# The low-part matmuls of an input projection, run between the high-part matmuls of the next weight unit

## The chip, the cores and the metric

The kernel runs on one core of one Trainium2 chip. The metric is the device time of one execution in microseconds (us). Three executions of the kernel before the change took 1726.51 to 1726.67 us, with a median of 1726.62 us.

## The reference

The kernel computes one decoder block in fp32 for a single sequence of 256 tokens and a model width of 2048. Two feed-forward layers of width 5632, each added at half weight, stand around a mixer. The mixer has two branches, a gated linear recurrence (LRU) and a short gated convolution, and both take their columns from one input projection `w_in` of 2048 x 5120.

```python
x = x + 0.5 * swiglu_ffn(rms_norm(x, ffn1_norm), ffn1_w_gate, ffn1_w_up, ffn1_w_down)
z = rms_norm(x, mix_norm) @ w_in                  # 256 x 2048 @ 2048 x 5120
lru_x, lru_gate, sc_b, sc_c, sc_x = split(z, 5)   # 1024 columns each
xc = causal_depthwise_conv(lru_x, lru_conv_w) + lru_conv_b
h = rg_lru(xc, lru_w_a, lru_b_a, lru_w_i, lru_b_i, lru_lambda)   # two 128x128 gates per head, then a scan
y_lru = h * gelu(lru_gate)
y_sc = sc_b * causal_depthwise_conv(sc_c * sc_x, sc_conv_w)
y = concatenate([rms_norm(y_lru, lru_out_norm), rms_norm(y_sc, sc_out_norm)])
x = x + y @ w_out
x = x + 0.5 * swiglu_ffn(rms_norm(x, ffn2_norm), ffn2_w_gate, ffn2_w_up, ffn2_w_down)
return rms_norm(x, final_norm)
```

The change touches the second line alone.

## The kernel before

**Products in parts.** Every fp32 product is made of passes in the format fp32r. A weight tile is split into a high part, which ScalarE (ACT) rounds to fp32r in two casts of 128x1024, and a low part, which VectorE (DVE) computes as raw minus high in one subtraction of 128x2048. The activations are split the same way. What is summed is high x high, high x low and low x high.

**Units.** A unit is 4 k-tiles of 128 rows by 512 columns of a weight: one load of 1 MB (`load`, L185, issued on SyncE's DMA queue), one pair of tiles for its parts (`split_tiles`, L198, from the pool `splits` of L78 with two buffers for high and two for low), the casts and the subtraction (`parts_of`, L214). The raw tiles come from the pool `raws` with three buffers (L81). `unit` (L221) is load and split together.

**The input projection.** `columns` (L331) computes 512 columns of z, transposed: the weight block is stationary, and the activations move. Four PSUM banks `ps_in`, one for each group of 128 columns, are filled from four units, 2048 rows in all. The activation tile `xT[u]` (called `xT_nm` in the profile) has 512 columns for each k-tile: the 256 tokens' high part and, beside it, their low part. So one high-part matmul moves 512 columns and gives high x high in the first half of the bank and high x low in the second; a low-part matmul moves the first 256 columns only and adds low x high to the first half. The two halves are added when the bank is emptied (`halves`, L992, and the additions after it). A unit has 16 high-part matmuls (4 k-tiles x 4 banks) and 16 low-part matmuls; before the change, all 16 high ones run and then all 16 low ones.

**The order of the columns.** The loop at L1216 calls `columns` eight times, by the list `order` of L1210: `in_0_0`, `in_0_1`, `in_1_0`, `in_4_0`, `in_1_1`, `in_4_1`, `in_2_0`, `in_2_1`. The function named in the list (`lru_x`, `lru_gate`, `sc_x`, `sc_b`) empties the four banks after each call. The 1024 columns of sc_c aren't made by `columns`: between the first and the second call stands a square product in seven products instead of eight (`sc_c`, L1145, through `seven`, L417; its tiles are named `in_c`). Its units of `w_in` are added to and subtracted from each other by DVE before they are split, and the parts of these go through the same two-buffered pool, except that every third pair of tiles comes from another pool there (L201). The products themselves are written by `multiply` (L228). Its results are copied out by `snap` (L443, the tiles `v_snap` and others) and combined on DVE. The emptying of the first call's banks (`half_x`, then the convolution in `xc`) is written behind its third product, by `between`.

**What lies between units.** Small pieces of later work (gates, convolutions, norms) are put on a list with a cost (`defer`, L61), and `pump(1.9)` at the end of each unit in `columns` lets pieces out until 1.9 us are spent. In the first call, the piece let out behind unit 0 holds the transposes of the last eight 128x128 blocks of the activations (`pt_nm`). In the second call, `first` runs behind unit 0 what the square product left to do (`turn`, L1153). A piece can hold small matmuls of its own, such as those of the LRU gates (`tha`, `thi` are ACT's reading of their banks).

**Who decides the order.** TensorE runs its instructions in the order written. For DVE and ACT a scheduler reorders within what the dependences allow, when the kernel is built; only the DMA issues on SyncE are held in the order written (L58, `sp.held`). Each engine then works through its queue in order. All eight PSUM banks come from one rotating pool (L83). All instructions go through one wrapper, so that the profile gives L43 as the line of almost all of them; tiles are told apart by their names.

Of the kernel before, what the change touches and what calls it, by code (L numbers as in the profile page):

```python
# [16 lines left out]
P = 128  # L17
D = 2048
S = 256
FF = 5632  # L20
NT = S // P
KD = D // P
KF = FF // P
CW = 512
NC_D = D // CW
UK = 4
# [23 lines left out]
def hybrid_block(ctx: ExitStack, tc: tile.TileContext, a: dict, out: bass.AP):  # L50
    nc = tc.nc
    Engine.pinned = False
    dve, act, pe, sp = (Engine(tc, e) for e in (nc.vector, nc.scalar, nc.tensor, nc.sync))
    sp.held = True
    x = a["x"][0]
# [12 lines left out]
    def pump(budget):  # L68

        owed[0] = min(owed[0], 0.0) + budget  # L70
        while pending and owed[0] > 0:
            cost, fn = pending.popleft()
            fn()
            owed[0] -= cost
# [10 lines left out]
    def bank(name):  # L85
        return psum.tile([P, 512], F32, tag="ps", name=name)
# [98 lines left out]
    def load(src, name, pieces=((0, UK),), loaded=None, kept=False):  # L185
        if kept and extra[0] is not bigs:
            raw = extra[0].tile([P, UK, CW], F32, tag="kept", name=f"raw_{name}", bufs=2)
        elif kept:
            raw = bigs.tile([P, UK, CW], F32, tag="big", name=f"raw_{name}")
        else:  # L190
            raw = raws.tile([P, UK, CW], F32, tag="raw", name=f"raw_{name}")
        for i, e in pieces:
            sp.dma_start(raw[:, i:e, :], src[i * P : e * P].rearrange("(j p) c -> p j c", p=P))
            if loaded:
                loaded(i)
        return raw

    def split_tiles(name):  # L198
        pool, bufs = splits, 2
        if extra:  # L200
            turn_of["split"] += 1  # L201
            if turn_of["split"] % 3 == 0:
                if extra[0] is bigs:
                    return [big(f"{part}_{name}") for part in ("hi", "lo")]
                pool, bufs = extra[0], 1
        return [pool.tile([P, UK, CW], F32R, tag=part, name=f"{part}_{name}", bufs=bufs) for part in ("hi", "lo")]

    def low_part(raw, hi, lo):
        dve.tensor_tensor(lo, raw, f32(hi), op=ALU.subtract)

    def blocks(hi, lo):
        return [(hi[:, j, :], lo[:, j, :]) for j in range(UK)]

    def parts_of(raw, name):  # L214
        hi, lo = split_tiles(name)
        for h in (slice(0, 2), slice(2, UK)):
            act.copy(hi[:, h, :], raw[:, h, :])
        low_part(raw, hi, lo)
        return blocks(hi, lo)

    def unit(src, name):  # L221
        return parts_of(load(src, name), name)
# [107 lines left out]

    def columns(w, c0, xT, name, first=None):  # L331
        ps = [bank(f"ps_{name}_{f}") for f in range(4)]
        for u in range(KD // UK):
            blk = unit(w[u * UK * P : (u + 1) * UK * P, c0 : c0 + CW], f"{name}_{u}")
            for part in range(2):
                for j in range(UK):
                    x = xT[u][:, j, :]
                    for f in range(4):
                        wf = blk[j][part][:, f * P : (f + 1) * P]
                        if part == 0:  # L340
                            pe.matmul(ps[f], wf, x, start=u == 0 and j == 0, stop=False)
                        else:
                            end = u == KD // UK - 1 and j == UK - 1
                            pe.matmul(ps[f][:, :S], wf, x[:, :S], start=False, stop=end)
            if u == 0 and first:
                first()
            pump(1.9)
        return ps
# [3 lines left out]
    def product(w, c, us, y, name, stagger=False, between=None):  # L352
        ps = [bank(f"ps_{name}_{t}") for t in range(NT)]
        cs = slice(c * CW, (c + 1) * CW)
        late = []
        for i, u in enumerate(us):
            blk = unit(w[u * UK * P : (u + 1) * UK * P, cs], f"{name}_{u}")
            begin, end = i == 0, i == len(us) - 1
            if stagger and i >= len(us) - 2:
                late.append((u, blk, begin, end))  # L360
            else:
                multiply([(ps[t], stationary(y(u), t), begin, end) for t in range(NT)], blk)
            if between:
                between(i)
            pump(1.5)

        for t in range(NT):
            for i, (u, blk, begin, end) in enumerate(late):
                if t < NT - 1:
                    multiply([(ps[t], stationary(y(u), t), begin, end)], blk)  # L370
                elif not end:
                    multiply([(ps[t], stationary(y(u), t), begin, i == len(late) - 2)], blk)
                else:
                    for o in (slice(0, CW // 2), slice(CW // 2, CW)):
                        ps.append(bank(f"ps_{name}_last")[:, : CW // 2])
                        multiply([(ps[-1], stationary(y(u), t), True, True)], [(h[:, o], l[:, o]) for h, l in blk])
        return ps
# [4 lines left out]
    def seven_of(sf, x0, x1, v, spare, parts, meanwhile=None):  # L382

        a11, a12, a21, a22 = v[0, 0], v[0, 1], v[1, 0], v[1, 1]
        parts = dict(zip((4, 5, 6, 2), parts))
        quads = {4: spare, 5: a11, 6: a21, 2: a12}
        sf.update({0: stationary(x0, 0), 1: stationary(x1, 0), 3: stationary(x1, 1)})

        def high(i):
            hi, lo = parts[i]
            act.copy(hi, quads[i])
            sf[i] = [(hi[:, j, :], lo[:, j, :]) for j in range(UK)]

        def low(i):
            hi, lo = parts[i]
            dve.tensor_tensor(lo, quads[i], f32(hi), op=ALU.subtract)

        def two():  # L400
            dve.tensor_tensor(a21, a11, a21, op=ALU.subtract)
            dve.tensor_tensor(a11, spare, a11, op=ALU.subtract)

        def last():
            dve.tensor_tensor(a12, a12, a11, op=ALU.subtract)

        dve.tensor_tensor(spare, a21, a22, op=ALU.add)
        high(4)
        if meanwhile:
            meanwhile()  # L410
        low(4)
        return two, last, high, low
# [4 lines left out]
    def seven(w, rows, cols, sf, xs, name, keep, done, between=None, early=False, own=None, factor=None):  # L417
# [33 lines left out]
        def product_of(i, raw, ps, begin=False, end=True, blk=None):  # L451
            multiply([(ps, sf[i], begin, end)], blk or parts_of(raw, f"{name}_p{i}"), True)

        def usual(i, raw, n, *targets, first=None):

            blk = first or parts_of(raw, f"{name}_x{i}{n}")
            if own:
                last = i == len(xs) - 1
                targets = [(apart[t, n], t, i == 0, last) for t in range(NT)]
            multiply([(ps, stationary(xs[i][1], t), b, z) for ps, t, b, z in targets], blk, True)  # L460
            if own and last:
                for t in range(NT):
                    own(t, n, apart[t, n])
# [509 lines left out]
    with tc.tile_pool(name="mixer", bufs=1, side="left") as mp, tc.tile_pool(name="mixw", bufs=2, side="left") as mw:  # L973
# [242 lines left out]
        for i, (use, part, half) in enumerate(order):  # L1216
            ps = columns(w_in, part * (D // 2) + half * CW, nm.xT, f"in_{part}_{half}", behind)
            behind = None
            if i == 0:
                flush()  # L1220
                nm.factor()
                nm.diagonals()
                nm.rows()
                bc = nm.bc
                behind = sc_c(lambda: use(ps, half))
                gate_weights("a", a["lru_w_a"][0])
                gate_weights("i", a["lru_w_i"][0])
                yT += [big(f"yT_{u}") for u in range(KD // UK)]
            else:
                use(ps, half)  # L1230
# [11 lines left out]
        for g in range(2):  # L1242
            if g == 1:
                flush()
            ps = product(w_out, 0, (2 * g, 2 * g + 1), yT.__getitem__, f"o0_{g}")
# [11 lines left out]
    with tc.tile_pool(name="outs", bufs=1, side="left") as op:  # L1257
# [10 lines left out]
        two, last_sum, high, low = seven_of(so, yT[0], yT[1], quads, spare, halves_of)  # L1268
# [9 lines left out]
        for g in range(2):  # L1278
            ps = product(
                w_out, 3, (2 * g, 2 * g + 1), yT.__getitem__, f"o3_{g}",  # L1280
                between=lambda i: [fn() for fn in steps[g, i]],
            )
# [122 lines left out]
```

## Time and profile before

| what | value |
|---|---|
| median of 3 executions | 1726.62 us |
| lowest and highest | 1726.51 and 1726.67 us |
| span of the profiled execution | 1725.0 us |
| what lies between the span and the median | 1.62 us |
| input projection with the square product, on TensorE | 705.8 to 933.9 us of the span |
| high-part matmuls of `columns` | 512, moving 512 columns each |
| low-part matmuls of `columns` | 512, moving 256 columns each |
| high-part casts on ACT (`hi_in`) | 64, 1045 ns each |
| low-part subtractions on DVE (`lo_in`) | 32, 2288 ns each |

The profile is one execution taken by the hardware profiler. PE is TensorE's matmuls, PEld its weight loads, which run beside the matmuls; DVE, ACT and POOL are VectorE, ScalarE and GpSimd, and SP is SyncE. An entry such as `ps_in<-xT_nm,lo_in x512` is a group of instructions by what they write and read, and how many they are. In a timeline, each row is a run of like instructions on an engine: start in us from the start of the span, length from the first start to the last end, engine, line, operation and tiles, shapes and count; a bracket gives the idle time before the row and what ended it. The recorded duration of a matmul includes its way through the array and overlaps the next one's, so that the step from one matmul to the next is read from starts, not from durations.

### The profile page before, as it was taken

The numbers are of one execution on the slowest core, as the hardware profiler recorded it, in microseconds if no ns is written. First come the engines' busy times: TensorE is split into PE (matmuls) and PEld (weight loads), VectorE is DVE, ScalarE is ACT, GpSimd is POOL, SyncE is SP. The second block draws the span as 40 slices with busy tenths as digits, with TensorE's granted clock in tenths as the row PEclk, the third lists the DMA queues.
The fourth block names the chain that finished last, engine by engine and source line by source line (L and its number), as shares of the span: only waits on it lengthen the run. The fifth ranks groups of instructions, "written<-read, shape, count | busy, mean of one in ns | idle before, by whom it ended". The sixth has DMA issues, their size and how long they took to land.

```text
span 1725.0 us, 20330 instructions
## 1 busy us (share of the span) xinstructions
PE 1715.1 (99%) x7985; PEld 1432.9 (83%) x7985; DVE 1509.3 (87%) x1239; ACT 1077.6 (62%) x1406; POOL 7.0 (0%) x34
## 2 busy tenths in 40 slices
PE   9999999999999999999999999999999999999998
PEld 8888888888888888888888888888888888888886
DVE  7998999889789898787897989889899887899896
ACT  7666566656466656666965657655556654656664
POOL 0100000000000000000000000000000000000000
PEclk9999999999999999999999999999999999999999
DMA  8574665566466656545566574665665646555743
GB/s 302 190 243 140 208 229 185 207 226 219 157 217 198 202 178 219 195 154 190 175 196 205 190 241 140 204 233 192 205 213 195 220 146 220 195 195 195 256 150 131
DMA packets 174223, 343.22 MB, mean 199 GB/s; under 512 B 5684, under 2 KB 8624, under 8 KB 174000
## 3 DMA queue, kind: packets, MB, share of 16 engines
q1 hardware_dynamic: 173632, 340.81, 58.5%
q8 instruction: 62, 1.02, 0.2%
q10 hardware_dynamic: 176, 1.06, 0.2%
q14 instruction: 33, 0.27, 0.0%
q0 software_dynamic: 320, 0.07, 0.0%
HBM read 339.82 MB, written 2.10 MB: 198 GB/s over the span
## 4 chain that ended last, share of the span: by engine, by line
PE 99%; DVE 0%; ACT 0%; DVEq 0%; issue 0%; ACTq 0%
PE ps_d L43 14%; PE ps_in L43 10%; PE ps_g_a L43 9%; PE ps_u_a L43 9%; PE ps_u_c L43 6%; PE ps_g_c L43 6%; PE ps_d_a L43 5%; PE ps_u_d L43 5%; PE ps_g_d L43 5%; PE ps_d_c L43 3%; PE ps_u_e L43 3%; PE ps_g_e L43 3%; PE ps_g L43 3%; PE ps_o L43 3%; PE ps_u L43 3%; PE ps_d_d L43 3%
## 5 line engine op out<-in xcount | busy, mean ns | idle before, releaser
L43 ACT CAST hi_g_p<-raw_g 128x1024 fp32r<-128x1024 f32 (+1 forms) x139 | 142.5, 1057 | 104.9 <-DVE raw_g L43 34.2
L43 DVE TENSOR_TENSOR lo_g_p<-raw_g,hi_g_p 128x2048 fp32r<-128x2048 f32 x70 | 159.5, 2285 | 31.6 <-ACT hi_g_p L43 31.3
L43 ACT CAST hi_u_p<-raw_u 128x1024 fp32r<-128x1024 f32 x140 | 141.4, 1050 | 68.1 <-DVE raw_u L43 24.7
L43 DVE TENSOR_TENSOR lo_u_p<-raw_u,hi_u_p 128x2048 fp32r<-128x2048 f32 x70 | 159.2, 2285 | 18.8 <-ACT hi_u_p L43 18.3
L43 PE MATMUL ps_d<-hi_d,h 128*128 128x512 f32 x696 | 166.0, 390 | 0.0
L43 PEld LDWEIGHTS ps_d<-hi_d,h 128*128 128x128 f32 x696 | 130.0, 188 | 26.6
L43 ACT CAST hi_d<-raw_d 128x1024 fp32r<-128x1024 f32 x88 | 88.6, 1048 | 68.3 <-PE ps_u_d L43 20.2
L43 DVE TENSOR_TENSOR lo_d<-raw_d,hi_d 128x2048 fp32r<-128x2048 f32 x44 | 100.6, 2289 | 28.9 <-ACT hi_d L43 28.9
L43 ACT CAST hi_d_p<-raw_d 128x1024 fp32r<-128x1024 f32 x84 | 85.3, 1050 | 61.2 <-DVE raw_d L43 42.2
L43 PE MATMUL ps_in<-xT_nm,hi_in 128*128 128x512 f32 x512 | 122.5, 391 | 0.0
L43 PEld LDWEIGHTS ps_in<-xT_nm,hi_in 128*128 128x128 f32 x512 | 94.1, 188 | 18.8 <-ACT tha L43 0.5
L43 ACT CAST hi_g_x<-raw_g 128x1024 fp32r<-128x1024 f32 (+1 forms) x79 | 81.5, 1059 | 39.4 <-PE ps_g_c L43 24.8
L43 ACT CAST hi_u_x<-raw_u 128x1024 fp32r<-128x1024 f32 x80 | 80.5, 1047 | 36.5 <-PE ps_u_c L43 20.0
L43 DVE TENSOR_TENSOR lo_d_p<-raw_d,hi_d_p 128x2048 fp32r<-128x2048 f32 x42 | 95.6, 2285 | 6.0 <-ACT hi_d_p L43 5.8
L43 DVE TENSOR_TENSOR raw_u<-raw_u,raw_u 128x2048 f32<-128x2048 f32 x40 | 91.6, 2289 | 9.5 <-DMA raw_u<-in_ffn_w_up_dram 8.8
L43 DVE TENSOR_TENSOR raw_g<-raw_g,raw_g 128x2048 f32<-128x2048 f32 x40 | 91.5, 2286 | 7.2 <-DMA raw_g<-in_ffn_w_gate_dram 6.8
L43 DVE TENSOR_TENSOR lo_g_x<-raw_g,hi_g_x 128x2048 fp32r<-128x2048 f32 x40 | 91.3, 2284 | 6.7 <-ACT hi_g_x L43 6.5
L43 DVE TENSOR_TENSOR lo_in<-raw_in,hi_in 128x2048 fp32r<-128x2048 f32 x32 | 73.2, 2288 | 26.5 <-ACT hi_in L43 26.0
L43 DVE TENSOR_TENSOR lo_u_x<-raw_u,hi_u_x 128x2048 fp32r<-128x2048 f32 x40 | 91.4, 2284 | 0.3
L43 PE MATMUL ps_d<-lo_d,h 128*128 128x512 f32 x348 | 86.2, 389 | 0.0
L43 ACT CAST hi_in<-raw_in 128x1024 fp32r<-128x1024 f32 x64 | 64.0, 1045 | 24.9 <-PE ps_in L43 15.4
L43 PEld LDWEIGHTS ps_d<-lo_d,h 128*128 128x128 f32 x348 | 65.3, 188 | 13.6
(471 smaller groups left out, 3737.6 us busy)
## 6 DMA issues: line engine op xcount, KB each, us to landing
raw_d<-in_ffn_w_down_dram SPq DMA_DIRECT2D x88, 1024.0 KB, 5.2
raw_u<-in_ffn_w_up_dram SPq DMA_DIRECT2D x87, 1024.0 KB, 5.3
raw_g<-in_ffn_w_gate_dram SPq DMA_DIRECT2D x86, 1024.0 KB, 5.3
raw_in<-in_w_in_dram SPq DMA_DIRECT2D x32, 1024.0 KB, 5.1
raw_in_c<-in_w_in_dram SPq DMA_DIRECT2D x8, 1024.0 KB, 5.3
raw_o<-in_w_out_dram SPq DMA_DIRECT2D x8, 1024.0 KB, 5.2
raw_o_q<-in_w_out_dram SPq DMA_DIRECT2D x8, 1024.0 KB, 5.2
xres<-in_x_dram SPq DMA_DIRECT2D x3, 512.0 KB, 9.3
```

The source lines that it names most:

```text
L43: ins = getattr(self.engine, name)(*args, **kwargs)
```

## The change

In `columns`, the sixteen low-part matmuls of a unit no longer follow its own sixteen high-part matmuls. They are held back and run between the high-part matmuls of the next unit: high 1 of unit u, low 1 of unit u-1, high 2 of unit u, low 2 of unit u-1, and so on. Unit 0's high-part matmuls run alone, since there is no unit before them, and the low part of unit 3 runs alone at the end. The number of matmuls, their operands and the loads stay the same. The calls of `first` and `pump` stay at the end of each unit's step, so that what they issue behind unit 0 now comes ahead of unit 0's low-part matmuls. Nothing is changed in the square product or in the other products, and the pools keep their sizes; `parts_of` is cut in two so that the tiles can be used as they are.

```diff
-    def parts_of(raw, name):
+    def split(raw, name):
         hi, lo = split_tiles(name)
         for h in (slice(0, 2), slice(2, UK)):
             act.copy(hi[:, h, :], raw[:, h, :])
         low_part(raw, hi, lo)
-        return blocks(hi, lo)
+        return hi, lo
+
+    def parts_of(raw, name):
+        return blocks(*split(raw, name))
+
+    def whole(src, name):
+        return split(load(src, name), name)
...
     def columns(w, c0, xT, name, first=None):
         ps = [bank(f"ps_{name}_{f}") for f in range(4)]
-        for u in range(KD // UK):
-            blk = unit(w[u * UK * P : (u + 1) * UK * P, c0 : c0 + CW], f"{name}_{u}")
-            for part in range(2):
-                for j in range(UK):
-                    x = xT[u][:, j, :]
-                    for f in range(4):
-                        wf = blk[j][part][:, f * P : (f + 1) * P]
-                        if part == 0:
-                            pe.matmul(ps[f], wf, x, start=u == 0 and j == 0, stop=False)
-                        else:
-                            end = u == KD // UK - 1 and j == UK - 1
-                            pe.matmul(ps[f][:, :S], wf, x[:, :S], start=False, stop=end)
+        n = KD // UK
+        before = []
+
+        def high(u, hi):
+            for j in range(UK):
+                x = xT[u][:, j, :]
+                for f in range(4):
+                    pe.matmul(ps[f], hi[:, j, f * P : (f + 1) * P], x, start=u == 0 and j == 0, stop=False)
+                    yield
+
+        def low(u, lo):
+            for j in range(UK):
+                x = xT[u][:, j, :S]
+                for f in range(4):
+                    end = u == n - 1 and j == UK - 1
+                    pe.matmul(ps[f][:, :S], lo[:, j, f * P : (f + 1) * P], x, start=False, stop=end)
+                    yield
+
+        for u in range(n):
+            hi, lo = whole(w[u * UK * P : (u + 1) * UK * P, c0 : c0 + CW], f"{name}_{u}")
+            for _ in high(u, hi):
+                if before:
+                    next(before[0])
+            before = [low(u, lo)]
+            if u == n - 1:
+                for _ in before[0]:
+                    pass
             if u == 0 and first:
                 first()
             pump(1.9)
```

## The prediction

> **What bounds the kernel now.** I read the page first: the span, the busy shares and the chain that ended last.
>
> ```profile
> span 1725.0 us, 20330 instructions
> PE 1715.1 (99%) x7985; PEld 1432.9 (83%) x7985; DVE 1509.3 (87%) x1239; ACT 1077.6 (62%) x1406; POOL 7.0 (0%) x34
> ...
> PE 99%; DVE 0%; ACT 0%; DVEq 0%; issue 0%; ACTq 0%
> ```
>
> TensorE is the path from end to end. Whatever the change does, it does by shortening the step from one matmul to the next, or by making TensorE wait. The profiled span of 1725.0 us lies 1.62 us under the median of the runs, 1726.62 us; I work out a difference against the span and add it to the median.
>
> Next the view by tile of the projection's PSUM tiles. Columns: shortest/median/longest in ns, then first and last start.
>
> ```profile
> L43 PE MATMUL ps_in<-xT_nm,hi_in x512: 387/389/499, 705.8 to 931.8; 128*128 128x512 f32 x171
> L43 PEld LDWEIGHTS ps_in<-xT_nm,lo_in x512: 187/192/192, 709.2 to 933.7; 128*128 128x128 f32 x171
> L43 PE MATMUL ps_in<-xT_nm,lo_in x512: 277/283/283, 709.4 to 933.8; 128*128 128x256 f32 x171
> ```
>
> These durations overlap, so they are not steps. A step is read from the timeline of PE (start us, length of the merged row, count), as the distance between starts of rows:
>
> ```profile
> 704.00 1.98 PE L43 MATMUL ps_d<-lo_d,h 128*128 128x512 f32 x8
> 705.81 3.79 PE L43 MATMUL ps_in<-xT_nm,hi_in 128*128 128x512 f32 x16
> 709.44 2.08 PE L43 MATMUL ps_in<-xT_nm,lo_in 128*128 128x256 f32 x16
> 711.35 1.04 PE L43 MATMUL pt_nm<-ident,xres 128*128 128x128 f32 x8
> 712.14 3.90 PE L43 MATMUL ps_in<-xT_nm,hi_in 128*128 128x512 f32 x16
> ...
> 717.79 3.82 PE L43 MATMUL ps_in<-xT_nm,hi_in 128*128 128x512 f32 x16
> 721.45 2.08 PE L43 MATMUL ps_in<-xT_nm,lo_in 128*128 128x256 f32 x16
> 723.36 3.82 PE L43 MATMUL ps_in<-xT_nm,hi_in 128*128 128x512 f32 x16
> 727.01 2.07 PE L43 MATMUL ps_in<-xT_nm,lo_in 128*128 128x256 f32 x16
> 728.93 0.60 PE L43 MATMUL pb_nm<-diag_nm,ones 128*128 128x128 f32 x4
> ...
> 732.11 1.98 PE L43 MATMUL ps_in_c_c<-hi_in_c_p,xis 128*128 128x512 f32 x8
> ...
> 742.99 1.07 PE L43 MATMUL ps_in_c_a<-lo_in_c_p,xis 128*128 128x512 f32 x4
> ```
>
> After 512-wide work a run of 16 high matmuls takes 709.44 - 705.81 = 3.63 us, 227 ns a step; after a low run it takes 721.45 - 717.79 = 3.66. A run of 16 low ones takes 1.91, 119 ns a step. Every low part is there when its run begins: no row waits for DVE.
>
> **The change part by part.**
>
> **1. The matmuls themselves.** None is added or removed: 512 high and 512 low. In each of the eight calls of columns, units 1 to 3 become 16 pairs (high, then a low one of the unit before): 8 x 3 x 16 = 384 pairs. Unit 0's high run and unit 3's low run stay unbroken. A pair costs 227 + 119 = 346 ns if the steps only change places. Two small effects of a switch are in the trace; I looked at the first six high matmuls after a low run (shortest/median/longest), and at the first low one after a high run (count, busy us, mean ns):
>
> ```profile
> L43 PE MATMUL ps_in<-xT_nm,hi_in x6: 389/394/398, 900.5 to 901.7; 128*128 128x512 f32 x6
> ```
>
> ```profile
> L43 PE MATMUL ps_in<-xT_nm,lo_in 128*128 128x256 f32 x1 | 0.3, 278 | 0.0
> ```
>
> After a low run the first high matmuls are 5 ns longer in the median and at most 398 - 389 = 9; the first low matmul after a high run is 283 - 278 = 5 ns shorter. In a pair both switches happen each time. From both sides: a pair loses at most 9 ns (384 x 9 = 3.5 us) and gains at most 283 - 277 = 6 (2.3 us). I take zero: the measured loss of 5 and gain of 5 cancel. What is sure is that 24 of the high runs that follow a low run go: 24 x (3.66 - 3.63) = 0.7 us, less the short first low matmul of each, 24 x 0.005 = 0.1. So -0.6 us.
>
> **2. The low buffers.** This is the larger term. High and low parts have two buffers each. A unit's low matmuls now end one unit later, so its low buffer comes free that much later: for unit 2, at the end of unit 3's high matmuls instead of before them. DVE takes its work in order and now waits longer. In the columns this has cover: a low part is also needed later, in its own unit's successor. It has none where another stage follows at once, and that is the square product after the first call (in_c), whose first low part uses unit 2's low buffer. DVE's timeline there:
>
> ```profile
> 720.49 2.28 DVE L43 TENSOR_TENSOR lo_in_c_x<-raw_in_c,hi_in_c_x 128x2048 fp32r<-128x2048 f32 x1
> 723.68 2.29 DVE L43 TENSOR_TENSOR lo_in_c_p<-raw_in_c,hi_in_c_p 128x2048 fp32r<-128x2048 f32 x1 [0.90 <-ACT hi_in_c_p L43]
> 726.00 4.62 DVE L43 TENSOR_TENSOR raw_in_c<-raw_in_c,raw_in_c 128x2048 f32<-128x2048 f32 x2
> 730.54 0.42 DVE L43 COPY bc_nm<-pb_nm 128x256 f32<-128x256 f32 x1
> 730.87 2.28 DVE L43 TENSOR_TENSOR lo_in_c_p<-raw_in_c,hi_in_c_p 128x2048 fp32r<-128x2048 f32 x1
> 733.07 0.75 DVE L43 TENSOR_TENSOR half_x<-ps_in,half_x 128x256 f32<-128x256 f32 x2
> ...
> 740.32 2.28 DVE L43 TENSOR_TENSOR lo_in_c_p<-raw_in_c,hi_in_c_p 128x2048 fp32r<-128x2048 f32 x1
> ```
>
> From 723.68 to 740.32 + 2.28 = 742.60 DVE runs without a gap: three low parts and three differences of the square product, bc, the eight small operations that empty the column's banks, six of xc (the last of these stand in the rows left out). The third low part ends 0.39 us before TensorE uses it (742.99). In the changed kernel's built order the same work stands between the first and the third low part, so the third ends as much later as the first begins.
>
> When does the first begin? Unit 0's high run ends at 709.44; the eight transposes, which now follow it directly, take 712.14 - 711.35 = 0.79; three units of pairs take 3 x (3.66 + 1.91) = 16.7. That gives 726.9. Unit 2's last low matmul starts one step earlier and runs 0.28: its buffer is free at 727.1. Before, DVE began at 723.68, when ACT had the high part. So DVE is 3.45 us later, the third low part ends at 746.05, and TensorE, which is at its old place (726.9 + 1.91 = 728.8 against 728.93), comes 3.45 - 0.39 = **3.1 us late**. On the way it stops twice already, and these stops are inside the 3.1: the second product's high part, cast by
>
> ```profile
> 728.40 2.00 ACT L43 CAST hi_in_c_p<-raw_in_c 128x1024 fp32r<-128x1024 f32 x2 [4.76 <-DVE raw_in_c L43]
> ...
> 732.31 0.69 ACT L43 ACTIVATE v_snap<-ps_in_c_a,r 128x512 f32<-128x512 f32 x1 [0.81 <-PE ps_in_c_a L43]
> ```
>
> now stands behind v_snap in ACT's order: 732.9 plus half of 2.00 is 733.9, against TensorE's need at 732.1. Its low part follows two differences later. After the third low part the square product's parts lie further ahead, and TensorE, being the bound, gets nothing back. Price from both sides: 0 if TensorE found other work for all of it (the built order brings only eight high matmuls forward, 1.8 us, and I counted DVE's end, which they do not change), 3.45 with no slack. I take 3.1.
>
> **3. High parts and evacuations.** A unit's high part is needed 1.91 us earlier, since the low run ahead of it is gone; its buffer comes free when it did. ACT casts it in 2.00 us and had 1.91 + 5.57 us; it has 5.57. Covered, also beside the gates. The gates and transposes that are issued between units come 1.91 us earlier too, on banks that are free. SP's loads keep their order and wait for the low parts' reading of the raw tiles, one unit later. By the page's row of DMA issues (count, KB, us from issue to landing)
>
> ```profile
> raw_in<-in_w_in_dram SPq DMA_DIRECT2D x32, 1024.0 KB, 5.1
> ```
>
> a load lands in 5.1 us, less than a unit's 5.57, and is read more than a unit later. At a column's start TensorE already waits a little for the banks of the last gate: the run
>
> ```profile
> 843.95 3.98 PE L43 MATMUL ps_in<-xT_nm,hi_in 128*128 128x512 f32 x16
> ```
>
> is 0.16 longer than the 3.82 of an undisturbed one. ACT now reaches that gate behind two half copies instead of one: I add 0.1 for each of the two columns that begin so, 0.2 in all.
>
> **Sum**: -0.6 + 3.1 + 0.2 = +2.7; three waits on TensorE each restart a high run, three times 0.03, +0.1. **+2.8 us on 1725.0, and 1726.6 + 2.8 = 1729.4 us.** That is 0.16%; what a measurement of this kernel can tell from no change is about 0.2%, 3.45 us, so the forecast lies just inside that bound.
>
> **The rivals.**
>
> *Pairs lose* (slower). If each high matmul behind a low one keeps the 9 ns, 3.5 us are added: 1732.9. For it speaks that such lengthening stands behind every low run; against it that it dies out within six matmuls, and that it may need a whole low run to arise. It carries the time past the 0.2% from 2 ns a pair on (3.45 - 2.8 = 0.65 us over 384 pairs).
>
> *DVE falls behind in the full columns* (slower). The busy time of DVE in two columns (stretch, length, busy):
>
> ```profile
> 797.07:819.36 22.29, 22.20 (x30) 1.00 0.47 148
> ...
> 843.95:866.92 22.97, 22.19 (x31) 1.00 0.46 142
> ```
>
> There is 0.1 and 0.8 us of room. Should the later buffers make DVE idle for one low part's wait in each, about a microsecond apiece, TensorE would wait as long: 1731.4. Against it: I find a low part ready 1.2 us or more ahead of its use in the built order.
>
> *Pairs gain* (not slower). A low matmul's weights, whose load is recorded at 192 ns (the PEld row above), are now loaded under a 512-wide one, with 227 ns instead of 119 to do it in. If the low step falls by 6 ns throughout, 2.3 us go: 1727.1. If weights were what a low step waits for, it could lose all above half a high step, 119 - 113.5 = 5.5, which is the same. The Trainium skill, "TensorE: Matmul & The Clock Gate", Back-to-back issue gap, gives a warm matmul's step as N/2.4 + 2.5 ns; by that a low step could fall to 109, an estimate, and the time to about 1725.5. The trace does not bear it out: by that rule a high step would be 216, and with 227 ns to load in it is 227.
>
> *The square product does not wait* (faster with gaining pairs). If something in the order frees DVE earlier, the 3.1 fall away, and with a gain of 6 ns a pair the time is 1724.0, or less if the step falls further.
>
> **How the numbers follow.** Forecast 0.55, spread over about 1 us each way, so 0.33 of it within 0.2% and 0.22 above. Pairs lose 0.15 and DVE behind 0.13, both slower by more than 0.2%. Pairs gain 0.12, within. No wait 0.05, counted as faster. So faster 0.05, same 0.45, slower 0.50. The range reaches from gaining pairs, 1727.0, to losing pairs with a little more, 1733.5.
>
> **What would show it.** Right: in the changed profile the first low part of in_c starts near 727.2 on DVE, PE shows idle time released by ACT and DVE between 732 and 747 that adds up to some 3 us, and a unit of pairs takes 5.5 to 5.6 us. Wrong: units of pairs of under 5.48 or over 5.7 us, waits on low parts in the columns after 775, or no gap in the square product.

## The result and the profile after

The changed kernel took 1732.68 us in the median of eight runs (1731.66 to 1734.87). The kernel before, run beside it, took 1727.69 us (eight runs, 1726.51 to 1728.86, the three that the forecast started from among them). The ratio is 1.003, with a 95% interval of 1.0021 to 1.0038: the change costs 5.2 us, between 3.6 and 6.6. The forecast was 1729.4 us, 2.8 over before, in a range of 1727.0 to 1733.5. The measured time lies inside the range and on the forecast side, near the upper end.

The page of the changed kernel, span, busy shares and the chain that ended last:

```profile
span 1730.5 us, 20333 instructions
PE 1718.0 (99%) x7985; PEld 1432.9 (83%) x7985; DVE 1509.6 (87%) x1239; ACT 1076.8 (62%) x1406; POOL 7.0 (0%) x34
...
PE 97%; DVE 2%; DMA 0%; issue 0%; ACT 0%; DVEq 0%; ACTq 0%
```

The span is 5.5 us longer. The matmuls are the same 7985. Of the chain, 2% now go through VectorE, where it was TensorE alone.

To see where the 5.5 us are, the start of each stage is read from TensorE's timeline and the distances are compared. The first call and the square product are taken from their first matmul to their last, the other calls from their start to the start of the next one, and `in_2_1` to its last matmul:

| stage on TensorE | before, us | after, us | difference |
|---|---|---|---|
| first call of columns (in_0_0), start to last matmul | 22.99 | 23.26 | +0.27 |
| square product (in_c), first to last matmul | 41.57 | 45.01 | +3.44 |
| in_0_1 | 25.99 | 26.23 | +0.24 |
| in_1_0 | 22.45 | 22.54 | +0.09 |
| in_4_0 | 24.43 | 24.66 | +0.23 |
| in_1_1 | 23.15 | 23.25 | +0.10 |
| in_4_1, in_2_0, in_2_1 | 22.27, 22.27, 22.15 | 22.52, 22.52, 22.40 | +0.25 each |
| all else (start and what follows the projection) | | | +0.39 |

The columns make 1.68 us, the square product 3.44. The last row isn't the change's: what follows the projection is the same code in all the kernels of this study, and took 782.5 to 783.3 us in them, from the last low matmul to TensorE's last one, but for one (`narrow_high`, below).

TensorE's timeline of the changed kernel, from the end of the first call to the third product's low part, answers to the one shown for before:

```profile
729.04 0.60 PE L43 MATMUL pb_nm<-diag_nm,ones 128*128 128x128 f32 x4
729.40 2.08 PE L43 MATMUL ps_in_c_a<-hi_in_c_p,xT_nm 128*128 128x512 f32 x8
731.31 1.07 PE L43 MATMUL ps_in_c_a<-lo_in_c_p,xT_nm 128*128 128x512 f32 x4
734.09 1.19 PE L43 MATMUL ps_in_c_c<-hi_in_c_p,xis 128*128 128x512 f32 x4 [1.71 <-ACT hi_in_c_p L43]
735.12 0.40 PE L43 MATMUL ps_in_c_e<-hi_in_c_x,xT_nm 128*128 128x512 f32 x1
735.35 1.07 PE L43 MATMUL ps_in_c_c<-hi_in_c_p,xis 128*128 128x512 f32 x4
736.26 1.75 PE L43 MATMUL ps_in_c_e<-hi_in_c_x,xT_nm 128*128 128x512 f32 x7
737.85 1.07 PE L43 MATMUL ps_in_c_e<-lo_in_c_x,xT_nm 128*128 128x512 f32 x4
739.00 1.20 PE L43 MATMUL ps_in_c_c<-lo_in_c_p,xis 128*128 128x512 f32 x4
740.97 2.09 PE L43 MATMUL ps_in_c_c<-hi_in_c_x,xT_nm 128*128 128x512 f32 x8 [0.78 <-ACT v_snap L43]
...
746.52 0.62 PE L43 MATMUL ps_in_c_a<-lo_in_c_p,xis 128*128 128x512 f32 x2
```

Two brackets name TensorE's gaps: 1.71 us for the second product's high part, and 0.78 us for v_snap, which reads out the second product's bank. Read from starts, against 226.7 ns a step, TensorE stops three times: 1.87 us before the second product's high part, 0.24 before its low part (739.00), and 0.95 for v_snap. The first step behind each stop is 0.11 longer as well, and together that is 3.4 us.

The rows show one thing more. Before the change, the second product's low part stood ahead of all matmuls of `ps_in_c_e`:

```profile
733.92 1.07 PE L43 MATMUL ps_in_c_c<-lo_in_c_p,xis 128*128 128x512 f32 x4
734.83 1.98 PE L43 MATMUL ps_in_c_e<-hi_in_c_x,xT_nm 128*128 128x512 f32 x8
```

Now it stands behind that bank's first twelve. The code of the square product is the same, so TensorE's order was rebuilt there too: that TensorE runs in the order written, as said above, holds for the matmuls of `columns` in both kernels, but not for the square product.

A bracket tells who came last. Why ACT was late stands one step further back, on VectorE, whose timeline is:

```profile
721.66 2.29 DVE L43 TENSOR_TENSOR lo_in<-raw_in,hi_in 128x2048 fp32r<-128x2048 f32 x1 [0.30 <-PE ps_in L43]
727.38 2.29 DVE L43 TENSOR_TENSOR lo_in_c_p<-raw_in_c,hi_in_c_p 128x2048 fp32r<-128x2048 f32 x1 [3.42 <-PE ps_in L43]
729.59 0.42 DVE L43 TENSOR_TENSOR half_x<-ps_in,half_x 128x256 f32<-128x256 f32 x1
729.92 0.41 DVE L43 COPY bc_nm<-pb_nm 128x256 f32<-128x256 f32 x1
730.25 2.28 DVE L43 TENSOR_TENSOR raw_in_c<-raw_in_c,raw_in_c 128x2048 f32<-128x2048 f32 x1
...
743.77 2.29 DVE L43 TENSOR_TENSOR lo_in_c_p<-raw_in_c,hi_in_c_p 128x2048 fp32r<-128x2048 f32 x1
```

VectorE stands still for 3.42 us, released by a matmul of `ps_in`: the last low one of unit 2, which frees the buffer. Behind the low part comes the difference at 730.25, which overwrites the raw tile that the low part has just read, so it can't go ahead of it. It ends at 732.53, and ACT casts its result at 733.00, behind v_snap. Some of this is the built order: half_x and bc stand ahead of the difference for 0.66 us (729.59 to 730.25), and v_snap holds the cast up for 0.47. By these rows, an estimate, 0.7 of the first stop's 1.87 us would be left without the two.

```profile
732.42 0.69 ACT L43 ACTIVATE v_snap<-ps_in_c_a,r 128x512 f32<-128x512 f32 x1 [2.34 <-PE ps_in_c_a L43]
733.00 1.99 ACT L43 CAST hi_in_c_p<-raw_in_c 128x1024 fp32r<-128x1024 f32 x2
```

The second cost is in the pairs of one high and one low matmul. In the column that starts at 893.84, TensorE's timeline reads:

```profile
893.84 4.04 PE L43 MATMUL ps_in<-xT_nm,hi_in 128*128 128x512 f32 x17
897.72 0.28 PE L43 MATMUL ps_in<-xT_nm,lo_in 128*128 128x256 f32 x1
897.83 0.40 PE L43 MATMUL ps_in<-xT_nm,hi_in 128*128 128x512 f32 x1
898.06 0.28 PE L43 MATMUL ps_in<-xT_nm,lo_in 128*128 128x256 f32 x1
...
898.78 0.28 PE L43 MATMUL ps_in<-xT_nm,lo_in 128*128 128x256 f32 x1
```

From 897.72 to 898.78 three pairs pass in 1.06 us, 353.3 ns each. No row has a gap. In the mean over all pairs the step behind a high matmul is 236.2 ns and the one behind a low matmul 117.1, where unbroken runs have 226.7 and 120.0: a pair takes 353.3 - 346.7 = 6.7 ns more.

### The profile page after: what moved, and what is told of

The parts are those of the page before. It is cut to its first block, busy times and chain, and to the rows that moved or that the text cites. A ratio compares the mean times of both kernels' runs of the same rounds, so it can differ in the third digit from the quotient of the medians.

```text
span 1730.5 us, 20333 instructions
## 1 busy us (share of the span) xinstructions
PE 1718.0 (99%) x7985; PEld 1432.9 (83%) x7985; DVE 1509.6 (87%) x1239; ACT 1076.8 (62%) x1406; POOL 7.0 (0%) x34
## 3 DMA queue, kind: packets, MB, share of 16 engines
q10 hardware_dynamic: 176, 1.06, 0.1%
## 4 chain that ended last, share of the span: by engine, by line
PE 97%; DVE 2%; DMA 0%; issue 0%; ACT 0%; DVEq 0%; ACTq 0%
PE ps_d L43 13%; PE ps_in L43 10%; PE ps_g_a L43 9%; PE ps_u_a L43 9%; PE ps_u_c L43 6%; PE ps_g_c L43 6%; PE ps_d_a L43 5%; PE ps_u_d L43 5%; PE ps_g_d L43 5%; PE ps_u_e L43 3%; PE ps_g_e L43 3%; PE ps_d_c L43 3%; PE ps_g L43 3%; PE ps_o L43 3%; PE ps_u L43 3%; PE ps_d_d L43 3%
## 5 line engine op out<-in xcount | busy, mean ns | idle before, releaser
L43 PE MATMUL ps_in<-xT_nm,hi_in 128*128 128x512 f32 x512 | 165.9, 397 | 0.0
L43 PE MATMUL ps_in<-xT_nm,lo_in 128*128 128x256 f32 x512 | 123.2, 281 | 0.0
L43 PEld LDWEIGHTS ps_in<-xT_nm,hi_in 128*128 128x128 f32 x512 | 95.8, 188 | 22.3
L43 PEld LDWEIGHTS ps_in<-xT_nm,lo_in 128*128 128x128 f32 x512 | 88.4, 189 | 0.6
```

What stands on the lines that cost most here:

```text
L43: ins = getattr(self.engine, name)(*args, **kwargs)
```

## The experiments

Two theories stood after the result. **Buffer and pairs**: the square product pays 3.44 us for one late low buffer, and the columns pay 6.7 ns a pair for the changing width of the matmuls. **Rivals**: the square product pays for the order of work that was rebuilt around it; the columns pay for waits on later buffers, for writing one bank twice in a row, for alternating tiles and weights, or for weight loads under a short matmul. The times below are medians beside a run of the kernel before on the same chip: 1727.39 us for the first four, 1727.54 for the others. The ratios, with their 95% intervals in brackets, aren't exactly those of the two medians. Stage times are read as in the table above.

### The low buffer given back early

```diff
-            if u == n - 1:
+            if u == n - 1 or (name, u) == ("in_0_0", n - 2):
                 for _ in before[0]:
                     pass
+                before = []
```

> In the first call alone, unit 2's low part runs unbroken behind its own high part, ahead of unit 3, as before the change; all else is the changed kernel. If the late low buffer is what the square product pays for, its stage on TensorE, 45.0 us in the changed kernel and 41.6 before, returns to 41.6, and the first low part of in_c starts on VectorE about 3.5 us earlier: 3.4 us under the changed kernel, some 1.8 us (0.1%) over the kernel before. If the stage pays for something else that the change moved (the order in which the first call's banks are emptied, the pieces let out earlier), it stays near 45.0 us and the time at 5 us (0.3%) over before.

Measured: 1729.19 us, ratio 1.0007 (0.9998 to 1.0015), 1.8 us over before. The square product takes 41.63 us. TensorE's timeline at the same place:

```profile
731.11 2.08 PE L43 MATMUL ps_in_c_a<-hi_in_c_p,xT_nm 128*128 128x512 f32 x8
733.02 1.07 PE L43 MATMUL ps_in_c_a<-lo_in_c_p,xT_nm 128*128 128x512 f32 x4
733.93 1.98 PE L43 MATMUL ps_in_c_c<-hi_in_c_p,xis 128*128 128x512 f32 x8
```

The second product follows the first without a bracket, and VectorE's first low part of the square product starts 18.2 us behind the projection's start (725.67 and 707.46) instead of 21.7. Since the position of unit 2's sixteen low matmuls is all that was put back (which leaves unit 3's high ones without a partner), and all other pairs stayed, the late low part behind unit 3 is what the square product paid for. The rebuilt order on TensorE and VectorE goes back with it, so this run alone doesn't tell whether the buffer or the order was the cause. The fifth one does.

### The low part delayed, without pairs

```diff
             for _ in high(u, hi):
-                if before:
-                    next(before[0])
+                pass
+            if before:
+                for _ in before[0]:
+                    pass
             before = [low(u, lo)]
```

> The low part of a unit still waits for the next unit's high part, but runs unbroken behind it: the buffers are held as long as in the changed kernel, and no pair is left. If the pairs themselves cost, each column's 0.1 to 0.3 us over before goes and the stages of columns return to 22.3 us, while the square product stays at 45.0 us: 3.4 us (0.2%) over before. If the columns are longer because of waits for the later buffers, they keep their 0.25 us each and the time stays at 5 us over before.

Measured: 1731.32 us, ratio 1.0021 (1.0012 to 1.0030), 3.9 us over before. The square product keeps its 45.01 us, and the columns are back at 22.25:

```profile
893.05 7.44 PE L43 MATMUL ps_in<-xT_nm,hi_in 128*128 128x512 f32 x32
900.34 2.08 PE L43 MATMUL ps_in<-xT_nm,lo_in 128*128 128x256 f32 x16
...
911.47 4.00 PE L43 MATMUL ps_in<-xT_nm,lo_in 128*128 128x256 f32 x32
915.30 0.86 PE L43 MATMUL ps_in<-xT_nm,hi_in 128*128 128x512 f32 x3
```

From 893.05 to 915.30 is 22.25 us, with the buffers held as long as in the changed kernel. The columns' loss is the pairs', not a wait.

### Groups of four

```diff
-            for _ in high(u, hi):
-                if before:
-                    next(before[0])
+            for i, _ in enumerate(high(u, hi)):
+                if before and i % 4 == 3:
+                    for _ in range(4):
+                        next(before[0])
```

> Four high matmuls, then four low ones of the unit before, instead of one and one. The square product stays at 45.0 us. If each change from low to high costs the 6.7 ns that a pair costs now (353.3 ns a pair against 346.6), a column has 12 such changes and takes about 22.3 us, as before: 3.4 us over before. If what is lost grows with the number of low matmuls ahead, up to the 21 ns that the trace of before shows for a run of sixteen, a column stays near 22.5 us: 5 us over before.

Measured: 1732.33 us, ratio 1.0024 (1.0015 to 1.0033). The column of the same place runs from 894.88 to 917.26 us and takes 22.38, between the two expectations of 22.3 and 22.5. Its timeline on TensorE, the first and the eleventh group of low matmuls:

```profile
899.45 0.64 PE L43 MATMUL ps_in<-xT_nm,lo_in 128*128 128x256 f32 x4
...
913.47 0.64 PE L43 MATMUL ps_in<-xT_nm,lo_in 128*128 128x256 f32 x4
```

Ten groups of four and four take 913.47 - 899.45 = 14.02 us, 1402 ns each, where unbroken runs would have 4 x 346.7 = 1387: 15 ns a group. In the kernel before, a run of sixteen low matmuls costs the high ones behind it about 28 ns and wins 7 at its first step, 21 in all. So the price of a change is 6.7 ns with one matmul each, 15 with four and 21 with sixteen. The price grows with the length of the runs, but neither of the two simple rules held.

### Another bank

```diff
-                for f in range(4):
+                for f in (2, 3, 0, 1):
                     end = u == n - 1 and j == UK - 1
```

> The low matmuls take the banks in the order 2, 3, 0, 1, so that a high matmul and the low one behind it never write the same PSUM bank. If writing one bank twice in a row is what a pair pays for, the pair falls from 353.3 to about 346.6 ns and the time by 2.6 us from the changed kernel's, to 2.8 us (0.16%) over before. If the change of width or of tiles is what it pays for, the pair stays at 353 ns and the time at 5 us over before.

Measured: 1732.93 us, ratio 1.0031 (1.0021 to 1.0041). The column takes 22.52 us as in the changed kernel, and the mean steps are 236.2 and 117.1 ns again. The bank has no part in it.

### Another pool for the first low part

```diff
             more_from(bigs)
+            turn_of["split"] = 2
             seven(
```

> The changed kernel, with one number moved: in the square product the first, fourth and so on pair of tiles comes from the other pool, instead of the third, sixth and so on, so that the first low part waits for no buffer of the first call. Those that do are needed later. If the wait for the late buffer at this one place is what the square product pays for, its stage returns from 45.0 to 41.6 us, or to at most 42.5 if the second operand's low part is now late, and the time to 1.8 us (0.1%) over before, with pairs still at 353 ns. If any order of buffers there gives the same queue on VectorE, the stage stays near 45 us and the time at 5 us over before.

Measured: 1729.27 us, ratio 1.0010 (1.0001 to 1.0019), 1.7 us over before. The square product takes 41.79 us. VectorE's timeline:

```profile
720.37 2.29 DVE L43 TENSOR_TENSOR lo_in_c_p<-raw_in_c,hi_in_c_p 128x2048 fp32r<-128x2048 f32 x1 [1.00 <-ACT hi_in_c_p L43]
722.58 2.29 DVE L43 TENSOR_TENSOR lo_in<-raw_in,hi_in 128x2048 fp32r<-128x2048 f32 x1
724.78 4.61 DVE L43 TENSOR_TENSOR raw_in_c<-raw_in_c,raw_in_c 128x2048 f32<-128x2048 f32 x2
729.31 2.28 DVE L43 TENSOR_TENSOR lo_in_c_p<-raw_in_c,hi_in_c_p 128x2048 fp32r<-128x2048 f32 x1
```

All pairs of the changed kernel are still there, and unit 2's buffer comes free as late as in it, 21.6 us behind the projection's start. The first low part goes ahead of the last one of the first call, and the differences start at 724.78 instead of 730.25. By the rotation in the code, the low part that now takes the late buffer is the second product's, at 729.31; it ends at 731.59, and TensorE uses it at 734.57. The line moves the high buffer of the first pair of tiles as well, but its cast began about as early in the changed kernel (721.59) as before (721.65), so that isn't what the change made late. The low buffer at that one place was the cause. How much of the 3.44 us is the bare wait, and how much the order that was built around it, no run separates, since the order was rebuilt in each.

### Both cures at once

The delayed kernel with the line of the run before.

> Both cures at once: the order of pools of the run before this, and the low part unbroken behind the next unit's high part, without pairs. If the change costs by these two terms and nothing else, columns take 22.3 us, the square product 41.6, and the time is that of the kernel before within 0.05% (1 us). If a third cost is left in the change, it shows here as a time over before by more than 0.1%.

Measured: 1727.57 us against 1727.54, ratio 0.9998 (0.9989 to 1.0007). The square product takes 41.61 us and the column 22.25. No third cost of more than 0.07% is left. It is no faster than the kernel before either, and no version here that does all the work was.

### Equal widths

Twice the matmuls of a pair were made equally wide: the low ones 512 wide, which adds the product of the two low parts, or the high ones of units 1 to 3 256 wide, which leaves out their product with the activations' low part.

```diff
-                x = xT[u][:, j, :S]
+                x = xT[u][:, j, :]
...
-                    pe.matmul(ps[f][:, :S], lo[:, j, f * P : (f + 1) * P], x, start=False, stop=end)
+                    pe.matmul(ps[f], lo[:, j, f * P : (f + 1) * P], x, start=False, stop=end)
```

> The low matmuls move 512 columns instead of 256: the product of the two low parts is added to the work, 512 x 107 = 55 us. Nothing changes width any more, while tiles and weights alternate as in the changed kernel. If the change of width is what a pair pays for, a pair takes 2 x 226.7 = 453 ns and the span is near 1783 us. If the alternation of tiles is, a pair takes 460 ns and the span is near 1785 us.

```diff
-                    pe.matmul(ps[f], hi[:, j, f * P : (f + 1) * P], x, start=u == 0 and j == 0, stop=False)
+                    if u:
+                        pe.matmul(ps[f][:, :S], hi[:, j, f * P : (f + 1) * P], x[:, :S], start=False, stop=False)
+                    else:
+                        pe.matmul(ps[f], hi[:, j, f * P : (f + 1) * P], x, start=j == 0, stop=False)
```

> The high matmuls of units 1 to 3 move 256 columns instead of 512: the product of the weights' high part with the activations' low part is left out in these units. Both widths are 256, and each weight load lies under a 256-wide matmul. If the change of width is what a pair pays for, the median pair takes 2 x 120 = 240 ns. If a weight load under a short matmul makes the next one late, or the alternation of tiles does, it takes 247 ns or more. The span says little: VectorE, with 22 us of work a column, then sets the columns' time.

Each was run once, and its time says little by itself (1781.96 and 1704.48 us); the steps answer. The timelines of TensorE, first with wide low matmuls, then with narrow high ones:

```profile
934.74 0.39 PE L43 MATMUL ps_in<-xT_nm,lo_in 128*128 128x512 f32 x1
934.97 0.39 PE L43 MATMUL ps_in<-xT_nm,hi_in 128*128 128x512 f32 x1
...
936.10 0.39 PE L43 MATMUL ps_in<-xT_nm,lo_in 128*128 128x512 f32 x1
```

```profile
867.69 0.28 PE L43 MATMUL ps_in<-xT_nm,lo_in 128*128 128x256 f32 x1
867.81 0.28 PE L43 MATMUL ps_in<-xT_nm,hi_in 128*128 128x256 f32 x1
...
868.89 0.28 PE L43 MATMUL ps_in<-xT_nm,lo_in 128*128 128x256 f32 x1
```

Three wide pairs take 936.10 - 934.74 = 1.36 us, 453 ns each; five narrow ones take 1.20 us, 240 ns each. Both are twice the step of an unbroken run, with tiles and weights alternating as before, and in the second case with every load under a short matmul. The loss needs the change of width. The wide kernel's span came to 1780.2 us where 1783 was expected: the expectation had kept the square product's 45 us, and it took 41.77. There the last low run of the first call takes 3.6 us instead of 1.9, and VectorE's first low part starts 3.74 us ahead of the square product (732.84 and 736.58) instead of 2.02. With narrow high matmuls TensorE waited for low parts in the columns, four times and 1.8 us in all, and 7.3 us at once in the output projection behind them; VectorE was busy for 93% of the time from 768 to 880 us. That VectorE alone set the columns' time, as expected, isn't shown.

## Why the prediction held, and where it didn't

**The low buffer: right, by place and chain.** The first low part was forecast for 727.1 and started at 727.38; the third was forecast to end at 746.05 and ended at 743.77 + 2.29 = 746.06. TensorE was forecast 3.1 us late and lost 3.44. The small miss is in how late TensorE may be before it waits: the third low part was ready 0.46 us before its use at 746.52, since the waits for the second product's high part and for v_snap had already cost as much. The decisive wait was the chain low part, difference, cast, and not the third low part's end; the prediction named this stop, with the high part ready at 733.9 where TensorE started it at 734.09, and took it for a part of the other. It also put the delay down to VectorE's order alone. The difference has to follow the low part in any order, because it overwrites its raw tile.

**The pairs: the failed step.** "I take zero: the measured loss of 5 and gain of 5 cancel." The runs show 6.7 ns lost a pair, 384 x 6.7 = 2.6 us; less the 0.6 us that the removed runs give back, as forecast, that is 2.0 us over the eight calls, 0.25 a call, where -0.6 was forecast. The bounds, 9 ns lost and 6 won, held. The value between them was wrong, because what the matmuls at the edges of long runs do was taken for what a pair does. The way of reading was not at fault. Taken from starts, the trace of before says the same as the durations did: the first high matmul behind a low run steps 233.4 ns in the mean, 6.7 over 226.7, and the first low one behind a high run 113.4, 6.6 under 120.0. In a pair the loss is greater and the gain smaller: a high matmul loses 236.2 - 226.7 = 9.5 and a low one wins 120.0 - 117.1 = 2.9. The kernel before has no such pair in `columns`, so its trace couldn't tell. A unit of pairs takes 16 x 353.3 = 5.65 us, over the 5.6 that was to show the forecast right and under the 5.7 that would have shown it wrong. The rival *Pairs lose* had this mechanism, at 9 ns, with a chance of 0.15.

**The column starts: wrong way.** 0.2 us were added for TensorE's waits at two starts. They went instead. TensorE's timeline of the changed kernel at the second of them, and ACT's reading of the last gate there, in the changed kernel and before:

```profile
848.07 3.82 PE L43 MATMUL ps_in<-xT_nm,hi_in 128*128 128x512 f32 x16
848.30 0.48 ACT L43 ACTIVATE thi<-pgate_i,hbi 128x256 f32<-128x256 f32 x1
844.16 0.47 ACT L43 ACTIVATE thi<-pgate_i,hbi 128x256 f32<-128x256 f32 x1
```

This run of sixteen takes the 3.82 us of an undisturbed one, where it had 3.98. The two columns (`in_1_0` and `in_1_1`) are longer by 0.09 and 0.10 us instead of 0.25, so that some 0.15 us each were won. The pairs have no part in it: in the delayed kernel, without pairs, the two are shorter than before, 22.25 and 22.98 us against 22.45 and 23.15. Nor is ACT ready earlier: it starts on the last gate 0.23 us behind the run's start now (848.30 and 848.07) and 0.21 before (844.16 and 843.95). The profile's names leave out which of the eight banks a tile has, so why TensorE no longer waits there stays open.

**The rest.** The rival *DVE falls behind in the full columns* didn't come: with the low part delayed and unbroken the columns take 22.25 us. *The square product does not wait* didn't either. For the gain of the rival *Pairs gain* nothing speaks: a low step fell to 117.1 ns in the mean, and the high step rose. Nor does anything speak for the N/2.4 + 2.5 ns that the Trainium skill ("TensorE: Matmul & The Clock Gate", Back-to-back issue gap) gives as the isolated gap of a warm matmul: by it, an estimate, a low step would be 109 ns, against 117.1 in the pairs and 120.0 in unbroken runs here.

The sum, then: 3.44 for the square product, 2.0 for the pairs, -0.3 for the starts, and 0.39 outside the projection, where two executions of the same code differ by as much: 5.5 us of span. The forecast's 2.8 us fall 2.7 short of it, and 2.6 of these are the pairs'. That the other misses (0.3, -0.5, -0.1 and 0.4) nearly cancel is luck. The range held because it reached to losing pairs.

## What to carry to other kernels

Run matmuls that move different widths in long runs, and not one by one, where TensorE is the bound: each change of width had a price here. When an order is changed so that a buffer is held longer, look for the place where another stage takes the next buffer of the same pool, and see whether its first need can go to another one; the steady loop can hide what the hand-over can't. What the first instruction of a long run does at its edge need not hold for a run of one: build the short run and measure its step.

## What the runs showed of the hardware

A change of width costs TensorE time that is not in the step of either width: 6.7 ns for one low and one high matmul, 15 for four and four, 21 for sixteen and sixteen, and nothing where the widths are equal (453 and 240 ns a pair). The loss falls on the high matmuls behind the low ones and is gone after five: behind sixteen low ones their steps are 233, 236, 228, 233 and 231 ns, and then 227. What causes it inside TensorE stays open. Two steps of unbroken runs, 226.7 ns for 512 columns and 120.0 for 256, differ by 106.7 ns for 256 columns. If a step grows evenly with the columns, which two widths can't show, that leaves 13.3 ns that belong to no column (120.0 - 106.7).
